# Retention: q of the last two heads made by seven-product jobs ahead, with the rotation of later k and q there

## The chip, the cores and the metric

The kernel runs on one core of a Trainium2 chip. The metric is the device time of one execution in microseconds. The core has a TensorE for matmuls (PE in the profile, PEld its weight loads), VectorE (DVE), ScalarE (ACT), GpSimd (POOL) and SyncE (SP), and 16 DMA engines. SP issues nearly all loads and stores, in its order; ScalarE and GpSimd have queues of their own.

## The reference

One inference step of a decoder with two layers: a short gated convolution with a SwiGLU, then retention with a SwiGLU. The change lies in the retention, which is computed for 512 prompt tokens and 32 sample tokens together (544 columns):

```python
def rotary(x, pos):                       # x1, x2: the two halves of 128
    return jnp.concatenate([x1 * cos - x2 * sin, x1 * sin + x2 * cos], axis=-1)

def retention_mixer(x, s0, pos, w_in, gn_g, w_out):
    q, k, v, g = jnp.split(x @ w_in, [QK_DIM, 2 * QK_DIM, 2 * QK_DIM + V_DIM], axis=-1)
    ...
    q = rotary(q, pos)
    k = rotary(k, pos) * (HEAD_DK ** -0.5)
    o, S = retention_chunkwise(q, k, v, s0)
    ...                                   # each head of o normalized: of
    out = (jax.nn.silu(g) * of) @ w_out
    return out, S
```

There are 4 heads; D_MODEL is 1024, a head has 256 columns of q and of k (two halves of 128 rows in the kernel) and 512 of v and of the gate g. Everything is float32.

## The kernel before

**Products.** Activations lie transposed, with channels on the partitions and 544 tokens along the free dimension. A float32 product is made of three matmuls on a high and a low part: high by high, high by low, low by high. `split` makes the parts, the high one by ScalarE (L204), the low one by VectorE (L205). A plain projection (`project`, L188) of 128 rows over 1024 channels has 8 channel tiles x 3 matmuls x 2 halves of 272 tokens: 48 matmuls. A projection of the retention's output (`held_project`) goes over one head's 512 channels, so it has 24.

**Seven-product jobs.** `Job` and `weights7` make a product of 256 rows by 1024 channels by 544 tokens with seven products of half size in place of eight: VectorE and ScalarE first form sums of the weights (L362 to L365, L337 to L339), GpSimd issues accumulating loads of low parts (L340), and `summed` adds the results up (ScalarE's copies for u1, u2 and p5, VectorE's additions L534 for c11, c12 and u3). A job has 7 x 4 x 3 = 84 matmuls of 272 columns (L424); as two plain projections it would be 96. `run` goes through a list of jobs; each prepares the weights of the next.

**Stages.** Convolution and its SwiGLU, up to 566 us; then `ahead`, which runs inside the end of that SwiGLU: it makes q and k of head 0 plainly, and then 11 jobs: the gates of all four heads (two jobs each) and k of heads 1, 2 and 3. What they make goes to DRAM (`qk_made`, `k_made`, `gate_made`) and is loaded back later. Work that a job leaves for later (`shaped`, the SiLU of a gate) is put in `pending` and issued at the next job's c11 (`flush`). Then come the four heads in turn, `last_project` and the second SwiGLU.

**A head.** `value` projects v (L1394 to L1396) in four groups; at group 1 it splits k and q of the head (`qk_split`) and, for heads 1 and 2, the gated output of the head before (`held_parts`). Then, woven by the order in which the loop of L1731 issues them and by `tc.issue_after`, which ties an issue behind an instruction: the loads of four sample-state tiles S (`states_load`), `state`, `scores`, `sample_outputs` (L1645), `states_update` (products L1663, VectorE's update L1669), `inner`, `normalized` and the gating (L1588). `fill(n)` puts the eight output projections of the older head between them, in pairs. While head h runs, its tail also makes q of head h + 1 by `qk_project` (two halves of 48 matmuls, each rotated as it comes out of PSUM, L1349), and rotates k of head h + 1 after its load (`rotate`, L1358 to L1366). Head 3 spreads the older head's projections over its own places and ends in `last_project`.

**Tiles.** `rot0` holds q, `rot1` holds k; `sqacc` and `sqlast` hold cos and sin; `qkhl1` is a tile of split parts; `gt`, `rot1`, `qkhl1` are reused in turn by the gate and by held parts. A tile can be written only when the last reader of what lay there is done.

## Time and profile before

| | us |
|---|---|
| median of 3 runs | 1382.14 (1382.0 to 1382.66) |
| span of the profiled execution | 1380.9 |
| TensorE busy | 1373.4 |
| VectorE busy | 1133.7 |
| `ahead`'s jobs | 566 to 682 |
| heads 0, 1, 2, 3 | from 682.0, 744.3, 831.4, 918.4 to 988.6 |

The span goes from the first to the last instruction of one execution on the chip that was taken with a profile. Engines run side by side, so an engine's busy time adds to the span only where nothing covers it. "Idle before, releaser" in a group's row says how long the engine had waited and for what. The chain of waits is followed back from the last instruction, step by step, to what released it.

### The profile page before, as it was taken

How to read it: one execution, taken by the hardware profiler on the slowest of the kernel's cores; microseconds unless marked ns; L12 is line 12 of the kernel's file. 1: busy time of each engine (PE TensorE's matmuls, PEld its weight loads, DVE VectorE, ACT ScalarE, POOL GpSimd, SP SyncE). 2: the span in 40 equal slices, each digit the busy share in tenths (PEclk: the TensorE clock that was granted, in tenths of full speed). 3: DMA queues.
4: the chain of work that ended last, by engine and by line, in shares of the span. 5: the costliest groups of instructions: out<-in, count | busy, mean ns of one | idle time of the engine just before them, and what ended most of it. 6: DMA issues, size and time to landing. Idle time of an engine off the chain costs nothing.

```text
span 1380.9 us, 26518 instructions
## 1 busy us (share of the span) xinstructions
PE 1373.4 (99%) x10420; PEld 1313.2 (95%) x10420; DVE 1133.7 (82%) x1929; ACT 822.6 (60%) x1288; POOL 212.1 (15%) x249
## 2 busy tenths in 40 slices
PE   9999999999999999999999999999999999999998
PEld 9999999999999999999978887887999999999998
DVE  6988889898989888777868576586799898989875
ACT  7666567677677656766631413224477767667654
POOL 0111011222222213211100000000112222221212
PEclk9999999999999999999999999999999999999999
DMA  6467347768676754777666455375757777777752
GB/s 225 121 157 169 110 108 172 171 165 187 145 191 151 166 123 128 189 202 208 189 231 229 146 186 205 134 260 184 225 126 161 171 177 171 157 180 164 166 112 88
DMA packets 99437, 232.89 MB, mean 169 GB/s; under 512 B 9808, under 2 KB 33888, under 8 KB 98928
## 3 DMA queue, kind: packets, MB, share of 16 engines
q1 hardware_dynamic: 68464, 167.26, 38.6%
q0 software_dynamic: 28400, 55.82, 23.4%
q10 hardware_dynamic: 2448, 8.12, 1.6%
q8 instruction: 81, 1.33, 0.4%
q14 instruction: 44, 0.36, 0.1%
HBM read 191.05 MB, written 28.42 MB: 159 GB/s over the span
## 4 chain that ended last, share of the span: by engine, by line
PE 99%; DVE 1%; issue 0%; DVEq 0%; ACT 0%
PE sm L424 45%; PE mm L424 16%; PE mm L188 16%; PE sm L188 6%; PE sm L1394 2%; PE sm L1395 2%; PE sm L1396 2%; PE sm L176 2%; PE sm L177 1%; PE sm L178 1%; PE sm L1645 1%; PE mm L1405 1%; PE mm L1573 1%; PE mm L1663 1%; PE sm L575 0%; PE mm L1464 0%
## 5 line engine op out<-in xcount | busy, mean ns | idle before, releaser
L424 PE MATMUL sm<-oh,wh 128*128 128x272 f32 x856 | 247.0, 289 | 0.0
L424 PE MATMUL sm<-ol,wh 128*128 128x272 f32 x856 | 246.2, 288 | 0.0
L424 PE MATMUL sm<-oh,wl 128*128 128x272 f32 x856 | 246.2, 288 | 0.0
L204 ACT ACTIVATE h<-w 128x512 fp32r<-128x512 f32 (+3 forms) x171 | 137.7, 805 | 90.5 <-PE mm L424 82.3
L205 DVE TENSOR_TENSOR l<-w,h 128x512 fp32r<-128x512 f32 (+3 forms) x171 | 154.6, 905 | 27.3 <-ACT h L204 25.1
L337 ACT ACTIVATE wh<-w 128x1024 fp32r<-128x1024 f32 (+1 forms) x133 | 132.9, 999 | 53.5 <-PE sm L424 40.0
L424 PEld LDWEIGHTS sm<-oh,wh 128*128 128x128 f32 x856 | 161.3, 188 | 0.6 <-DVE b L534 0.3
L424 PEld LDWEIGHTS sm<-oh,wl 128*128 128x128 f32 x856 | 161.1, 188 | 0.1
L424 PEld LDWEIGHTS sm<-ol,wh 128*128 128x128 f32 x856 | 160.8, 188 | 0.0
L424 PE MATMUL sm<-parts,wh 128*128 128x272 f32 x736 | 142.2, 288 | 0.0
L204 ACT ACTIVATE wh<-w 128x1024 fp32r<-128x1024 f32 (+3 forms) x80 | 69.0, 873 | 118.2 <-PE mm L188 61.2
L340 POOL DMA_DIRECT2D wl<-in_ffgu_dram x87 | 81.7, 939 | 323.5 <-ACT wl L339 136.7
L424 PEld LDWEIGHTS sm<-parts,wh 128*128 128x128 f32 x736 | 115.3, 188 | 0.0
L424 PE MATMUL mm<-oh,h 128*128 128x272 f32 x396 | 113.9, 288 | 0.0
L424 PE MATMUL mm<-oh,l 128*128 128x272 f32 x396 | 113.4, 286 | 0.0
L424 PE MATMUL mm<-ol,h 128*128 128x272 f32 x396 | 113.2, 286 | 0.0
L424 PE MATMUL sm<-parts,wl 128*128 128x272 f32 x368 | 106.0, 288 | 0.0
L339 ACT ACTIVATE wl<-wh 128x512 fp32r<-128x512 f32 (+1 forms) x172 | 102.4, 595 | 2.2
L338 DVE TENSOR_TENSOR wl<-w,wh 128x512 fp32r<-128x512 f32 (+1 forms) x133 | 86.3, 649 | 13.4 <-ACT wh L337 13.0
L205 DVE TENSOR_TENSOR wl<-w,wh 128x1024 fp32r<-128x1024 f32 (+3 forms) x80 | 81.2, 1023 | 14.5 <-ACT wh L204 14.1
L188 PE MATMUL mm<-parts,wh 128*128 128x272 f32 x488 | 82.8, 291 | 0.0
L424 PE MATMUL sm<-oh,h 128*128 128x272 f32 x284 | 82.8, 291 | 0.0
(384 smaller groups left out, 3816.1 us busy)
## 6 DMA issues: line engine op xcount, KB each, us to landing
w<-in_ffgu_dram SPq DMA_DIRECT2D x66, 512.0 KB
wl<-in_ffgu_dram POOLq DMA_DIRECT2D x87, 256.0 KB, 5.5
S<-in_rets_dram SPq DMA_DIRECT2D x16, 1024.0 KB
out_rets_dram<-S SPq DMA_DIRECT2D x16, 1024.0 KB
w<-in_ffdn_dram SPq DMA_DIRECT2D x36, 384.0 KB
cb<-in_ffgu_dram SPq DMA_DIRECT2D x22, 512.0 KB
w<-in_cvin_dram SPq DMA_DIRECT2D x21, 512.0 KB
wl<-in_ffdn_dram POOLq DMA_DIRECT2D x48, 192.0 KB, 4.7
```

What stands on the lines that cost most here:

```text
L176: nc.tensor.matmul(out, lh, rh, start=start, stop=False, skip_group_check=True)
L188: last_product[0] = nc.tensor.matmul(half(pt, hf)[:, :HT], w[:, c], act[k][:, hf * HT : (hf + 1) * HT], start=(first and k == ks[0] and i ...
L204: h = nc.scalar.activation(dh, src, AF.Copy)
L205: last_low[0] = nc.vector.tensor_sub(dl, src, dh.bitcast(F32))
L337: nc.scalar.activation(wh, w, AF.Copy)
L338: last_mixed[0] = nc.vector.tensor_sub(wl[:, :n], w[:, :n], wh[:, :n].bitcast(F32))
L339: minus = nc.scalar.activation(wl[:, n:], wh[:, n:].bitcast(F32), AF.Copy, scale=-1.0)
L340: nc.gpsimd.dma_start(wl[:, n:], src[:, 1, :] if len(src.shape) == 3 else src[:, n:], accum_op=ALU.add)
L424: last = nc.tensor.matmul(out, w[:, c], b, start=(first and j == 0 and i == 0), stop=(j == len(self.ks) - 1 and i == 2), skip_group_check= ...
L1394: nc.tensor.matmul(out, xh[kt][:, ts_], wh[:, cw], start=(kt == 0), stop=False)
L1395: nc.tensor.matmul(out, xh[kt][:, ts_], wl[:, cw], start=False, stop=False)
L1396: last = nc.tensor.matmul(out, xl[kt][:, ts_], wh[:, cw], start=False, stop=(kt == KT - 1))
```

## The change

- `ahead` runs 13 jobs instead of 11: q of heads 2 and 3 is now made by jobs of its own, (2, "q") and (3, "q"), and `qk_project` is called only in head 0, for q of head 1.
- k of heads 1 to 3 and q of heads 2 and 3 are rotated in `ahead` before they go to DRAM (`turn`, put in `pending`), with two temporaries from the pool `fp`. cos and sin are loaded after the first job. The mark `whole` stays only on the last two jobs.
- `sqacc` and `sqlast` become the halves of one tile, `squares`, which holds k of heads 2 and 3 once cos and sin are no longer needed.
- The gate of every head is loaded before `fill(2)`, from head 1 on into `qkhl1`. `held_parts` runs at group 1 of `value` for heads 1, 2 and 3 alike.
- The older head's projections stand singly in heads 1 and 2: 0, 1, 2, then 3 and 4; 5 in the place of q's first half, 6 in that of its second, and 7 behind it. Head 3 keeps its places.
- The made q of heads 2 and 3 is loaded at the end of the head before.

`rotate` and `turned` move up unchanged from the retention to a place ahead of `ahead`, and are left out here.

```diff
...
+QAHEAD = (2, 3)
...
-    sqacc = resid.tile([P, T], F32, tag="sqacc", name="sqacc")
-    sqlast = resid.tile([P, T], F32, tag="sqlast", name="sqlast")
+    squares = resid.tile([P, 2, T], F32, tag="squares", name="squares")
+    sqacc, sqlast = squares[:, 0, :], squares[:, 1, :]
...
     k_made = {h: dram.tile([P, 2, T], F32, tag=f"k{h}", name=nm("km")) for h in range(1, NH)}
+    q_made = {h: dram.tile([P, 2, T], F32, tag=f"q{h}", name=nm("qm")) for h in QAHEAD}
     gate_made = {h: dram.tile([P, 4, T], F32, tag=f"g{h}", name=nm("gm")) for h in range(NH)}
...
-            def k(what, src):
+            def qk(what, src):
                 g = tile2()
...
                     nc.scalar.activation(g[:, 1, :HT], src, AF.Copy)
-                    nc.scalar.dma_start(k_made[h], g)
-            if n is None:
-                return Job([a["rtqk"][h, 2 + i] for i in range(2)], operand, sw, summed(tile2, k), third, spare=spare(), first=0)
+                    def turn():
+                        two = [fp.tile([P, 5, HT], F32, tag="f", name=nm("rt")) for _ in range(2)]
+                        rotate(g, *[t[:, :2, :].rearrange("p a b -> p (a b)") for t in two])
+                        nc.scalar.dma_start((q_made if n == "q" else k_made)[h], g)
+                    pending.append(turn)
+            if n in ("q", "k"):
+                at = 2 * (n == "k")
+                return Job([a["rtqk"][h, at + i] for i in range(2)], operand, sw, summed(tile2, qk), third, spare=spare(), first=0)
-        jobs = [gates(*hn) for hn in ((0, 0), (0, 2), (1, None), (1, 0), (1, 2), (2, None), (2, 0), (2, 2), (3, None), (3, 0), (3, 2))]
+        jobs = [
+            gates(*hn)
+            for hn in (
+                (0, 0), (0, 2), (1, "k"), (1, 0), (1, 2), (2, "k"), (2, 0), (2, "q"), (2, 2), (3, "k"), (3, 0), (3, "q"), (3, 2)
+            )
+        ]
...
-        for one_job in (jobs[5], jobs[8], *jobs[-2:]):
+        for one_job in jobs[-2:]:
             one_job.places["whole"] = True
-        run(jobs, (2, 5, 6), lambda i: factors() if i == 1 else None, iter(()))
+        def after(i):
+            if i == 0:
+                with tc.issue_after(last_load[0].ins):
+                    for j, t in enumerate((cos, sin)):
+                        nc.sync.dma_start(t, a["rope"][j])
+            elif i == 1:
+                factors()
+        run(jobs, (2, 5, 6), after, iter(()))
...
-        cos, sin = sqacc, sqlast
-        for i, t in enumerate((cos, sin)):
-            nc.sync.dma_start(t, a["rope"][i])
...
-            return {"rot": [
-                pool.tile([P, 2, T], F32, tag=f"rot{w}", name=nm("rot"), bufs=1) for w, pool in enumerate((tp, kp))
-            ]}
+            rot = tp.tile([P, 2, T], F32, tag="rot0", name=nm("rot"), bufs=1)
+            return {"rot": [rot, squares if h in QAHEAD else kp.tile([P, 2, T], F32, tag="rot1", name=nm("rot"), bufs=1)]}
...
                 if c == 1:
-                    with tc.issue_after(last_normal[0].ins) if h else ExitStack():
-                        qk_split(h, st, 1)
+                    if h not in QAHEAD:
+                        with tc.issue_after(last_normal[0].ins) if h else ExitStack():
+                            qk_split(h, st, 1)
                     qk_split(h, st, 0)
...
                     keys(h, st, pvs[:, 1, P:])
-                    if h in AHEAD:
+                    if h:
                         held_parts(h, older)
+                    if h in QAHEAD:
+                        qk_split(h, st, 1)
...
         def held_parts(h, st):
-            if h in AHEAD:
-                yh = [kp.tile([P, 2, T], F32R, tag=t, name=nm("oldh"), bufs=1) for t in ("gt", "rot1")]
-                yl = swapped(h == 2, [P, 4, T], F32R, "oldl")
-                for i, t in enumerate(yh):
-                    c = slice(2 * i, 2 * i + 2)
-                    split(t, yl[:, c, :], st["gate"][0][:, c, :])
-                held["y"] = [t[:, n, :] for t in yh for n in range(2)], [yl[:, n, :] for n in range(4)]
-            else:
-                for n in range(4):
-                    split(xh[n], xl[n], gate_tile(st, n))
-                held["y"] = xh[:4], xl[:4]
+            yh = [kp.tile([P, 2, T], F32R, tag=t, name=nm("oldh"), bufs=1) for t in ("gt", "rot1")]
+            yl = swapped(h > 1, [P, 4, T], F32R, "oldl")
+            for i, t in enumerate(yh):
+                c = slice(2 * i, 2 * i + 2)
+                split(t, yl[:, c, :], st["gate"][0][:, c, :])
+            held["y"] = [t[:, n, :] for t in yh for n in range(2)], [yl[:, n, :] for n in range(4)]
...
-            def fill(n):
-                if h in AHEAD:
-                    for i in range(2):
-                        held_project(h, (0, 4, 2, 6)[n] + i)
-                        if n == i == 0:
-                            st["placed"]()
-                elif not more and n % 2:
-                    if n == 1:
-                        held_parts(h, older)
-                    held_project(h, 2 + n // 2)
+            def fill(place):
+                for n in {1: ((0,), (1,), (2,), (3, 4)), 2: ((0,), (1,), (2,), (3, 4)), 3: ((), (2,), (), (3,))}.get(h, ((),) * 4)[place]:
+                    held_project(h, n)
+                    if n == 0:
+                        st["placed"]()
...
                 scores(h, st, c)
-            if h == 0:
-                st["gate"] = [swapped(True, [P, 4, T], F32, "gate")]
-                nc.sync.dma_start(st["gate"][0], gate_made[0])
+            st["gate"] = [qp.tile([P, 4, T], F32, tag="qkhl1", name=nm("gate"), bufs=1) if h else swapped(True, [P, 4, T], F32, "gate")]
+            nc.sync.dma_start(st["gate"][0], gate_made[h])
             fill(2)
...
             first = first or [inner(h, st, it) for it in range(2)]
-            if h in AHEAD:
-                st["gate"] = [swapped(h == 2, [P, 4, T], F32, "gate")]
             if more:
...
                 states_load(h, st, 3)
-            if h in AHEAD:
-                with tc.issue_after(st["loaded"].ins):
-                    nc.sync.dma_start(st["gate"][0], gate_made[h])
-            elif not more:
-                st["gate"] = [
-                    pool.tile([P, 2, T], F32, tag=t, name=nm("gate"), bufs=1) for pool, t in ((qp, "qkhl1"), (kp, "gt"))
-                ]
-                for i, t in enumerate(st["gate"]):
-                    nc.sync.dma_start(t, gate_made[h][:, 2 * i : 2 * i + 2, :])
             yn0 = normalized(first[0], fe[:, 0, h : h + 1])
...
             states_update(h, st, 1)
-            if more:
-                with tc.issue_after(last_update[0].ins):
-                    rotate(nxt["rot"][1], *products())
             sample_outputs(h, st, 2)
...
             with tc.issue_after(last_product[0].ins):
-                if more:
+                if h == 0:
                     qk_project(h + 1, nxt, 0, 0)
                 else:
-                    held_project(h, 4)
+                    held_project(h, 5 if more else 4)
             with tc.issue_after(last_product[0].ins):
...
-            if more:
+            if h == 0:
                 qk_project(h + 1, nxt, 0, 1, inside)
+            elif more:
+                nc.sync.dma_start(nxt["rot"][0], q_made[h + 1])
+                held_project(h, 6, single=True, weave=(None, inside))
+                held_project(h, 7)
             else:
...
                 held_project(h, 0, False, single=True, weave=iter((inside,)))
```

The first order is VectorE's in `ahead`, around the job (2, "q"), whose result is gate_8047. Before, at the end of the job of k of head 2 (gate_7771), with sums of weights (w, L362 to L365) and low parts (wl, l) of later jobs:

```order
L534 TENSOR_TENSOR gate_7771<-gate_7771,mm_7842 128x272
L205 TENSOR_TENSOR l_939_7826<-w_931_7802,h_938_7825 128x512
L338 TENSOR_TENSOR wl_7940<-w_7930,wh_7939 128x512
L205 TENSOR_TENSOR l_950_7942<-w_945_7931,h_949_7941 128x1024
L534 TENSOR_TENSOR gate_7901<-gate_7901,sm_7986 128x272
```

After, at the end of the job of q of head 2:

```order
L536 TENSOR_TENSOR gate_8047<-gate_8047,mm_8118 128x272
L1117 TENSOR_TENSOR rt_8276<-gate_8047,squares 128x544
L207 TENSOR_TENSOR l_976_8102<-w_968_8078,h_975_8101 128x512
L1118 TENSOR_TENSOR gate_8047<-gate_8047,squares 128x544
L340 TENSOR_TENSOR wl_8215<-w_8205,wh_8214 128x512
L1119 TENSOR_TENSOR rt_8275<-gate_8047,squares 128x544
L1120 TENSOR_TENSOR gate_8047<-gate_8047,squares 128x544
L1124 TENSOR_TENSOR gate_8047<-gate_8047,rt_8275 128x544
L207 TENSOR_TENSOR l_987_8217<-w_982_8206,h_986_8216 128x1024
L536 TENSOR_TENSOR gate_8177<-gate_8177,sm_8261 128x272
L340 TENSOR_TENSOR wl_8225<-cb,wh_8224 128x512
L1125 TENSOR_TENSOR gate_8047<-gate_8047,rt_8276 128x544
```

The six operations of the rotation now stand between the splits of the next job's weights.

The second is VectorE's at the start of head 0, after the small operations of the setup (put is the last). Before, k of head 0 (rot_8571) has been rotated further up, and only its low part and the rotation of q (rot_8570) stand here:

```order
L1327 TENSOR_TENSOR put<-cb 128x128
L1215 TENSOR_TENSOR gate_8405<-gate_8405,R 128x1088
L205 TENSOR_TENSOR qkhl_8681<-rot_8571,qkhl_8681 128x1024
L1358 TENSOR_TENSOR rt_8602<-rot_8570,sqlast 128x544
L1360 TENSOR_TENSOR rt_8601<-rot_8570,sqlast 128x544
```

After, with k as rot_8867 and q as rot_8866:

```order
L1360 TENSOR_TENSOR put<-cb 128x128
L207 TENSOR_TENSOR wl_9024<-w_9022,wh_9023 128x1024
L1232 TENSOR_TENSOR gate_8699<-gate_8699,R 128x1088
L1117 TENSOR_TENSOR rt_1053_8883<-rot_8867,squares 128x272
L1119 TENSOR_TENSOR rt_1053_8883<-rot_8867,squares 128x272
L1118 TENSOR_TENSOR rot_8867<-rot_8867,squares 128x272
L1120 TENSOR_TENSOR rot_8867<-rot_8867,squares 128x272
L1124 TENSOR_TENSOR rot_8867<-rot_8867,rt_1053_8883 128x272
L1125 TENSOR_TENSOR rot_8867<-rot_8867,rt_1053_8883 128x272
L1117 TENSOR_TENSOR rt_8898<-rot_8866,squares 128x544
L1117 TENSOR_TENSOR rt_1054_8890<-rot_8867,squares 128x272
```

A split of value weights and the rotation of k in two halves now come ahead of the rotation of q.

The third place is the end of head 1. On TensorE, the values of head 2 (L1394 to L1396 before, L1415 to L1417 after) begin there. Before, they follow the last matmuls of q of head 2 (sm_9917, sm_9918):

```order
L188 MATMUL sm_9918<-parts,wh_9912 128x272
L188 MATMUL sm_9917<-parts,wl_9913 128x272
L188 MATMUL sm_9918<-parts,wl_9913 128x272
L1394 MATMUL sm_9990<-wh_9996,parts 128x512
L1395 MATMUL sm_9990<-wl_9997,parts 128x512
```

After, with L1597 as a transposition of normalized rows, L1687 as the two products of the last state tile (mm_10102, mm_10103), and sm_10080 and sm_10081 as the halves of projection 6 of the older head:

```order
L1597 MATMUL sm_10094<-cb,yn_10046 128x128 x4
L1687 MATMUL mm_10102<-vs_9713,kns_9582 128x512 x2
L190 MATMUL sm_10081<-oldh_9589,wh_10075 128x272
L190 MATMUL sm_10080<-oldl_9590,wh_10075 128x272
L1687 MATMUL mm_10103<-vs_9713,kns_9582 128x512 x2
L190 MATMUL sm_10081<-oldl_9590,wh_10075 128x272
L190 MATMUL sm_10080<-oldh_9589,wl_10076 128x272
L190 MATMUL sm_10081<-oldh_9589,wl_10076 128x272
L1415 MATMUL sm_10151<-wh_10157,parts 128x512
L1416 MATMUL sm_10151<-wl_10158,parts 128x512
```

Projection 6 ends there in place of q, with the products of the last state tile five matmuls before its end, and projection 7 follows after the first eight matmuls of the values.

On VectorE in the same tail, from the second update of state tile 2 on. Before (rot_9732 is k, rot_9731 q of head 2):

```order
L1669 SCALAR_TENSOR_TENSOR S_9388<-S_9388,mm_9903 128x1024
L1588 TENSOR_TENSOR gate_9730<-gate_9730,sm_9955 128x4x128
L1550 TENSOR_SCALAR yn_9961<-sm_9860,mv_9887,rs_9888 128x512
L1669 SCALAR_TENSOR_TENSOR S_9734<-S_9734,mm_9963 128x1024
L1669 SCALAR_TENSOR_TENSOR S_9734<-S_9734,mm_9964 128x1024
L1349 TENSOR_TENSOR rt_9845<-sm_9917,sqlast 128x272
L1349 TENSOR_TENSOR rt_9845<-sm_9918,sqlast 128x272
L1349 TENSOR_TENSOR rot_9731<-sm_9917,sqacc 128x272
L1349 TENSOR_TENSOR rot_9731<-sm_9918,sqacc 128x272
L1365 TENSOR_TENSOR rot_9731<-rot_9731,rt_9845 128x544
L1366 TENSOR_TENSOR rot_9731<-rot_9731,rt_9846 128x544
```

After (rot_9936 is the made q of head 2, x the residual):

```order
L1693 SCALAR_TENSOR_TENSOR S_9676<-S_9676,mm_10065 128x1024
L1612 TENSOR_TENSOR gate_9818<-gate_9818,sm_10094 128x4x128
L1574 TENSOR_SCALAR yn_10100<-sm_10022,mv_10049,rs_10050 128x512
L1693 SCALAR_TENSOR_TENSOR S_9938<-S_9938,mm_10102 128x1024
L1693 SCALAR_TENSOR_TENSOR S_9938<-S_9938,mm_10103 128x1024
L318 TENSOR_TENSOR x_80<-x_80,sm_10080 128x272
L318 TENSOR_TENSOR x_80<-x_80,sm_10081 128x272
L207 TENSOR_TENSOR qkhl_10231<-rot_9936,qkhl_10231 128x1024
L1444 SCALAR_TENSOR_TENSOR qm<-rot_9936,gs_10234 128x4x4 x3
L318 TENSOR_TENSOR x_81<-x_81,mm_10125 128x544
```

The rotation of q out of PSUM is gone, and the additions of projections 6 and 7 stand there.

More of the change, by code (lines that the diff above doesn't have):

```diff
@@ L1107, in hybrid_decode_kernel, with rotate, turned @@
     k_made = {h: dram.tile([P, 2, T], F32, tag=f"k{h}", name=nm("km")) for h in range(1, NH)}
+    q_made = {h: dram.tile([P, 2, T], F32, tag=f"q{h}", name=nm("qm")) for h in QAHEAD}
     gate_made = {h: dram.tile([P, 4, T], F32, tag=f"g{h}", name=nm("gm")) for h in range(NH)}
+    cos, sin = sqacc, sqlast
+    def rotate(r, t0, t1, c=slice(0, T)):
+        nc.vector.tensor_mul(t1, r[:, 0, :], sin[:, c])
+        nc.vector.tensor_mul(r[:, 0, :], r[:, 0, :], cos[:, c])
+        nc.vector.tensor_mul(t0, r[:, 1, :], sin[:, c])
+        nc.vector.tensor_mul(r[:, 1, :], r[:, 1, :], cos[:, c])
+        turned(r, t0, t1)
+    def turned(r, t0, t1):
+        nc.vector.tensor_sub(r[:, 0, :], r[:, 0, :], t0)
+        nc.vector.tensor_add(r[:, 1, :], r[:, 1, :], t1)
     def ahead(tp, fp, sw, operand_tiles, wp):
```

9 lines of the change are left out of this document (removed).

## The prediction

> **What bounds the kernel now.** I read the page's busy line and its chain first, to see which engine sets the end:
>
> ```profile
> PE 1373.4 (99%) x10420; PEld 1313.2 (95%) x10420; DVE 1133.7 (82%) x1929; ACT 822.6 (60%) x1288; POOL 212.1 (15%) x249
> PE 99%; DVE 1%; issue 0%; DVEq 0%; ACT 0%
> ```
>
> TensorE is busy for 1373.4 of 1380.9 us, and the chain that ends last lies on it for 99%. So time goes only if matmuls go, and time comes only if TensorE is made to wait. The list of waits, asked for TensorE alone, has one entry:
>
> ```profile
> PE sm L575 <- DVE expo L109: 1.1, 1, 1.1
> ```
>
> That wait is at the start of the program, far from the change. Then I cut the span by stage and by head (columns: sum of the stretch, busy time and count of PE, PEld, DVE, ACT, POOL, the granted clock, the DMA share, GB/s):
>
> ```profile
> 566.00:686.00 120.00, 120.00 (x940) 118.85 (x940) 89.11 (x149) 82.11 (x131) 17.91 (x24) 1.00 0.69 189
> ...
> 682.00:744.30 62.30, 62.30 (x366) 47.90 (x365) 47.90 (x83) 21.10 (x33) 7.58 (x13) 1.00 0.70 235
> 744.30:831.40 87.10, 87.10 (x566) 72.75 (x565) 60.76 (x95) 24.16 (x33) 2.65 (x5) 1.00 0.54 184
> 831.40:918.40 87.00, 87.00 (x565) 72.65 (x564) 60.80 (x95) 24.03 (x32) 2.65 (x5) 1.00 0.54 187
> 918.40:988.60 70.20, 70.20 (x430) 55.42 (x429) 51.79 (x90) 22.07 (x32) 3.62 (x6) 1.00 0.61 207
> ```
>
> The first row is the seven-product jobs of `ahead`, the others are heads 0 to 3. In all five TensorE has no gap. VectorE is at 74% in `ahead` and at 70% in heads 1 and 2: it is the engine that can fall behind.
>
> **The matmuls.** A busy time per matmul must not be used here, since neighbours overlap:
>
> ```profile
> L188 PE MATMUL mm<-parts,wh 128*128 128x272 f32 x160 | 26.9, 289 | 0.0
> ```
>
> 289 ns is what one takes from start to end. What a removed one gives back is the step from one to the next, and the chain has it (start, length, count): first three pieces of a seven-product job, then the two halves of q's projection, that of head 0 and that of head 1.
>
> ```profile
> 618.71 3.02 PE sm L424 x24
> 621.73 1.51 PE mm L424 x12
> 623.24 4.49 PE sm L424 x36
> ...
> 726.11 6.02 PE mm L188 x48
> ...
> 813.24 6.01 PE mm L188 x48
> ```
>
> A plain projection of one half of q is 48 matmuls in 6.02 us, 125.4 ns each. Heads 1 and 2 each lose two halves: 4 x 48 = 192 matmuls, 4 x 6.02 = 24.1 us. In the jobs 72 matmuls take 9.02 us, 125.3 ns each; a job has seven products of 12, so 84 matmuls and 10.52 us. Two are added: 168 matmuls, 21.0 us. **The path of TensorE gets shorter by 24 matmuls, 3.0 us.** The rest of its work is only placed anew: the eight projections of the older head stay 24 matmuls (3.0 us) each. The second half of q, which was woven with other work, hands its place to the projection `held_project` 6, of the same form, so what the weaving costs stays.
>
> The Trainium skill, page "TensorE: Matmul & The Clock Gate", section "Back-to-back issue gap", gives the isolated warm gap as N / 2.4 + 2.5 ns; for 272 columns my estimate by it is 115.8 ns, and the gain would be 2.8 us. The rows above show 125.4 ns, at a granted clock of 1.00, and the sum goes by them.
>
> **VectorE in `ahead`.** Five rotations come in here (k of heads 1 to 3, q of heads 2 and 3), six operations of 128x544 each. Before, one of them is on the timeline at the tail of head 1 (start, length):
>
> ```profile
> 812.91 0.72 DVE L1358 TENSOR_TENSOR rt<-rot,sqlast 128x544 f32<-128x544 f32 x1
> 813.55 0.72 DVE L1360 TENSOR_TENSOR rt<-rot,sqlast 128x544 f32<-128x544 f32 x1
> ...
> 816.09 0.71 DVE L1366 TENSOR_TENSOR rot<-rot,rt 128x544 f32<-128x544 f32 x1
> 816.73 0.69 DVE L1536 BATCH_NORM_STATS2 bst<-sm 128x6 f32<-128x512 f32 x1
> ```
>
> From 812.91 to 816.73: 3.8 us for one rotation, 19.1 us for five. The stage had 89.1 us of VectorE in 11 jobs, 8.1 us a job; two more bring 16.2 us, and the rotation of k of head 0, which leaves the stage, takes 4.2 us away. That is 120 us of VectorE in 141 us, 85%. It does not lie evenly: a job of q or k has 8.1 + 3.8 = 11.9 us of VectorE behind 10.5 us of TensorE and falls 1.4 us behind; the gate job after it has 8.1 us and regains 2.4. The cover is that order: apart from the first, every second job is one of gates. VectorE also had time to wait there:
>
> ```profile
> L534 DVE TENSOR_TENSOR gate<-gate,sm 128x272 f32<-128x272 f32 x22 | 9.5, 434 | 6.1 <-PE sm L424 5.8 <-ACT wl L339 0.3
> ```
>
> Its additions waited 5.8 us for TensorE, so it was ahead of it then. I take nothing here; without that reserve it is 5 x 1.4 = 7.0 us, and it can't be below nothing, since TensorE had no wait in this stage to lose. The stores of k and q go out on ScalarE's queue, and the added jobs' weights come on SP's and POOL's queues in their order and at the jobs' own pace of 10.5 us, as those of the other jobs did.
>
> **The start of head 0.** k of head 0 was loaded early and rotated on VectorE beside the last jobs, in 12 operations on half tiles from 668.8 to 674.1:
>
> ```profile
> 668.82 0.43 DVE L1358 TENSOR_TENSOR rt<-rot,sqlast 128x272 f32<-128x272 f32 x1
> 669.17 0.43 DVE L1360 TENSOR_TENSOR rt<-rot,sqlast 128x272 f32<-128x272 f32 x1
> ...
> 673.76 0.43 DVE L1366 TENSOR_TENSOR rot<-rot,rt 128x272 f32<-128x272 f32 x1
> ```
>
> Now its tile shares memory with a temporary of the rotation of q of head 3, and the load comes behind that. Its rotation then stands at the head's start, between these rows of before:
>
> ```profile
> 682.53 1.29 DVE L1215 TENSOR_TENSOR gate<-gate,R 128x1088 f32<-128x1088 f32 x1
> 683.74 1.22 DVE L205 TENSOR_TENSOR qkhl<-rot,qkhl 128x1024 fp32r<-128x1024 f32 x1
> 685.27 0.73 DVE L1358 TENSOR_TENSOR rt<-rot,sqlast 128x544 f32<-128x544 f32 x1 [0.32 <-DMA rot<-qkm]
> ...
> 688.46 0.72 DVE L1366 TENSOR_TENSOR rot<-rot,rt 128x544 f32<-128x544 f32 x1
> ...
> 695.56 0.19 DVE L1619 TENSOR_TENSOR ss<-mm,mput 128x32 f32<-128x32 f32 x1 [3.67 <-PE mm L1614]
> ```
>
> and on TensorE's chain:
>
> ```profile
> 694.99 0.46 PE mm L1614 x4
> ...
> 708.36 0.43 PE sm L176
> ```
>
> In the frame of before: a split of value weights (1.2 us) and the gate's product (1.2) end at 684.9; 12 operations on halves of k at 0.35 us from start to start make 4.2, q's rotation 3.8, the low part of k 1.1: q is ready at 694.1, where L1614 wants it at 695.0. Before, q was done at 689.2, with some 6 us to spare; now 0.9 are left. I take nothing. The bounds are nothing and 4.2 us, the whole rotation of k, if its load lands that late. Behind it on VectorE stand the low part of q (1.2 us) and the small operations for the sample states; the products that use them begin after the values, at 708 us, so a delay of 1 us there is covered.
>
> **The tails of heads 1 and 2.** Before, the stretch from the third state update to the next head's values was covered on TensorE by q's projection, 12.0 us; now by held projections 5, 6 and 7, 9.0 us. VectorE loses there one rotation of k and one of q (7.6 us) and gets three additions to the residual:
>
> ```profile
> L1669 DVE SCALAR_TENSOR_TENSOR S<-S,mm 128x1024 f32<-128x1024 f32 x32 | 38.1, 1211 | 1.2 <-PE mm L1663 1.2
> L316 DVE TENSOR_TENSOR x<-x,mm 128x544 f32<-128x544 f32 x19 | 13.7, 719 | 21.1 <-PE mm L188 21.1
> ```
>
> three at 0.72 us, 2.2 us. So VectorE is eased by 5.4 us and TensorE by 3.0; in sum the tail is not tighter. But single places are: the second product of state tile 2, the second normalization and both products of tile 3 now stand 2 to 4 us apart on TensorE, where VectorE has two updates of 1.2 us, a normalization and a gating of 0.7 us each between them. Adding these durations up in the order of both engines, I place each of these, as an estimate, within 0.1 to 0.4 us of its need. The price if one update is late is 1.2 us a head, 2.4 in all. On the other side, before, projections stood in pairs, the second waiting for the first's addition: two of them took 3.22 and 3.18 us instead of 24 x 0.1254 = 3.01:
>
> ```profile
> 771.29 3.22 PE mm L188 x24
> ...
> 775.44 3.18 PE mm L188 x24
> ```
>
> 0.2 us each, two such in both heads, 0.8 us at most to gain. I take +0.2 us, between these ends and near to nothing, since the large sums balance.
>
> **Loads, and head 3.** Heads 1 and 2 now last 75 us each. They moved 184 GB/s x 87.1 us = 16.0 MB; without q's weights (1.0 MB) and with the made q (0.6) it is 15.6 MB, 207 GB/s over 75 us; head 0 ran at 235. Two loads are placed anew on SP's queue. The gate (1.1 MB, 6 us at that rate) now stands ahead of the head's state tile 3, which used to go first: at most 6 us later, with no wait of TensorE for a state before. The made q stands behind the next head's state tile 0, and on VectorE the addition of projection 7 and the last gating wait behind its split. The nearest row is what the made k cost VectorE as a load in three heads:
>
> ```profile
> L1358 DVE TENSOR_TENSOR rt<-rot,sqlast 128x544 f32<-128x544 f32 x4 | 2.9, 722 | 2.2 <-DMA rot<-km 1.9 <-DMA rot<-qkm 0.3
> ```
>
> 1.9 us of VectorE, 0.6 a head, none of it on the path. For both I take nothing, with the price of a tail as their bound. Head 3 has one gating operation in place of two and splits its held tiles earlier: nothing to 0.5 us gained, I take nothing.
>
> **Sum.** 1380.9 - 24.1 + 21.0 + 0.2 = 1378.0 us of span. The median of the runs, 1382.14, is 1.24 us above the profiled span, so **1379.3 us**: 2.8 us less, 0.21%. About 0.2%, 2.8 us, is what a measurement of this kernel can tell from no change, so the forecast lies just at that edge.
>
> **Rivals.**
> - The lost cover turns into waits: one update late in both tails (2.4 us), or the start of head 0 late by its reserve again (0.9 us). For it: reserves of 0.1 to 0.9 us where there were 6 and more. Against it: VectorE's sum in the tails falls. It gives 1379.1 + 0.9 to 2.4, some 1380 to 1381.5: no difference that can be told. Chance 0.41.
> - VectorE becomes the bound in `ahead`, and it ends slower: each of the five q and k jobs is 1.4 us late because a rotation stands in front of a split that the next product needs, and the gate jobs do not win it back for TensorE. 1379.1 + 7.0 = 1386.1 us. It decides once the reserve of those splits is under 1.4 us. Against it are the 5.8 us of waiting above. Chance 0.08.
> - The start of head 0 is late by all of k's rotation, 4.2 us: 1383.3, on the edge of slower. Chance 0.04, half of it slower.
> - The rotations hold up POOL: both their inputs lie in SBUF. If each of 30 operations stopped POOL for its 0.72 us, its accumulating loads of low weights would come 21.6 us late in all, at most 1400.7 us. Chance 0.02. This is a rule of the Trainium skill (page "SBUF — State Buffer", section "Who interferes with whom": a two-input operation of VectorE from SBUF contends with GpSimd instructions that read SBUF); no row of before shows such a stop.
> - A removed matmul is worth its whole 289 ns: 24 x 0.289 = 6.9 us, 1375.2 us. The chain's 125 ns speak against it. Chance 0.02.
> - The change doesn't do what it says: the heads still hold q's products. The order shows them gone; no chance is given.
>
> **How the numbers follow.** The forecast (gain of 2.8 to 3.5 us) has 0.43, the waits 0.41, the rest 0.16 as above (0.01 of it for nothing named, slower). Faster by over 0.2%: 0.43 + 0.02 = 0.45; slower: 0.08 + 0.02 + 0.02 + 0.01 = 0.13; within: 0.42. The range starts at 1378.0 (1379.1 less 0.8 in the tails and part of head 3's 0.5) and ends at 1383.0 (1379.1 with 2.4 in the tails, 0.9 at head 0 and some more); it leaves out the 289 ns, the slower cases and a little of the waits, 2 in 10.
>
> **What would show it.** The jobs' stage is 21 us longer with TensorE busy throughout; heads 1 and 2 take 75.0 us each, head 0 62.3. Wrong would be (lines of the changed kernel): a wait of TensorE for the splits L340 or L207 in `ahead`; for the rotation L1124 or L1125 at L1638; for the update L1693 or the gating L1612 between a head's last state and the next value L1415; or chain pieces of 12 matmuls in `ahead` longer than 1.51 us.

## The result, and the profile after

| | before | changed kernel |
|---|---|---|
| median, us | 1382.4 (1382.0 to 1382.67, 4 runs) | 1393.34 (1392.58 to 1395.63, 4 runs) |
| span of the profiled execution | 1380.9 | 1391.8 |

The ratio is 1.008, 95% interval [1.0066, 1.0094]: slower by 10.9 us where 2.8 us less were forecast. The page of the changed kernel, busy line and chain:

```profile
PE 1376.3 (99%) x10396; PEld 1313.6 (94%) x10396; DVE 1141.3 (82%) x1938; ACT 832.5 (60%) x1304; POOL 216.0 (16%) x255
...
PE 96%; DVE 2%; DMA 1%; ACT 1%; issue 0%; SPq 0%; DVEq 0%; ACTq 0%
```

The 24 matmuls are gone (10420 to 10396 in the records). But TensorE holds 96% of the chain in place of 99%, and the list of waits of TensorE (us in total, times, longest) has new entries:

```profile
PE sm L426 <- ACT oh L206: 6.5, 3, 5.5
...
PE sm L426 <- DVE ol L207: 0.9, 2, 0.7
PE sm L1597 <- DVE yn L1574: 0.4, 2, 0.2
PE sm L1416 <- DVE wl L207: 0.2, 1, 0.2
```

L426 is the matmul of the seven-product jobs. To see which jobs, I cut both spans at the same events: the first matmul of `ahead`'s jobs, the first value matmul of each head, the first matmul of the last SwiGLU and its last seven-product matmul. The windows of before, the jobs of `ahead` and then head 3 and the last SwiGLU (length in us, then busy time and count of PE, PEld, DVE, ACT, POOL, the granted clock, DMA share, GB/s):

```profile
565.30:681.90 116.60, 116.60 (x929) 116.18 (x927) 86.05 (x145) 78.94 (x124) 13.97 (x17) 1.00 0.68 188
...
918.40:1018.70 100.30, 100.30 (x669) 85.45 (x668) 77.73 (x135) 48.31 (x68) 7.68 (x11) 1.00 0.64 197
1018.70:1345.90 327.20, 327.20 (x2620) 326.88 (x2619) 292.60 (x517) 225.51 (x358) 66.60 (x77) 1.00 0.71 161
```

And of the changed kernel, all stages:

```profile
564.70:702.10 137.40, 137.40 (x1097) 137.09 (x1096) 112.66 (x181) 91.11 (x145) 19.42 (x25) 1.00 0.73 195
702.10:764.50 62.40, 62.40 (x366) 47.87 (x366) 48.74 (x93) 21.94 (x34) 6.08 (x13) 1.00 0.67 236
764.50:837.80 73.30, 72.88 (x445) 57.82 (x444) 51.41 (x83) 21.95 (x30) 2.65 (x5) 1.00 0.58 201
837.80:913.70 75.90, 75.68 (x470) 60.98 (x468) 51.07 (x80) 22.15 (x30) 2.65 (x5) 1.00 0.57 203
913.70:1017.60 103.90, 103.71 (x693) 88.61 (x691) 67.72 (x107) 39.45 (x53) 7.94 (x11) 1.00 0.65 201
1017.60:1357.00 339.40, 332.11 (x2618) 330.39 (x2619) 301.88 (x535) 234.83 (x371) 66.33 (x76) 0.98 0.67 155
```

| stage, us | before | changed | difference |
|---|---|---|---|
| `ahead`'s jobs | 116.6 | 137.4 | +20.8 |
| head 0 | 62.4 | 62.4 | 0 |
| heads 1, 2, 3 and `last_project` | 274.4 | 253.1 | -21.3 |
| last SwiGLU, to its last seven-product matmul | 327.2 | 339.4 | **+12.2** |

The first two rows are as forecast (+21.0 and 0), the third should have been -23.9 (24.1 less the 0.2 for the tails). The fourth is a stage that the prediction does not mention, in which the change edits nothing.

What happened at its start is read from the chain of waits of the changed kernel (start, length, what):

```profile
990.44 23.73 PE mm L190 x189
1014.17 0.02 issue
1014.19 0.28 ACT wh L339
1014.47 0.69 issue
1015.15 0.73 ACT f L884
...
1021.80 2.47 DVE ol L207 x3
...
1029.12 0.64 DVE ol L207
1029.76 0.04 issue
1029.81 1.27 PE sm L426 x4
```

Before, the same chain goes from one matmul stage to the next without leaving TensorE:

```profile
991.96 26.95 PE mm L188 x215
1018.90 8.77 PE sm L424 x69
```

f (L884, L882 before) is the scratch tile in which the SwiGLU scales the residual and from which ScalarE and VectorE split the operands oh and ol of its first products. When it was written is a view of that one line (count, duration min/median/max, first and last start). Before, then the changed kernel:

```profile
L882 ACT ACTIVATE f<-x,vec x8: 733/737/752, 992.7 to 1020.7; 128x544 f32<-128x544 f32 x8
```

```profile
L884 ACT ACTIVATE f<-x,vec x6: 732/735/749, 1015.2 to 1024.0; 128x544 f32<-128x544 f32 x6
```

Before, the first operands were made beside the last projections, from 992.7 us on; now the first f comes at 1015.2, after `last_project` has last read the held parts (1014.2 on TensorE), and most of the operands are made on ScalarE and VectorE with TensorE waiting.

### The profile page after: what moved, and what is told of

The parts are those of the page before. It is cut to its first block, busy times and chain, and to the rows that moved or that the text cites. A ratio compares the mean times of both kernels' runs of the same rounds, so it can differ in the third digit from the quotient of the medians.

```text
span 1391.8 us, 26526 instructions
## 1 busy us (share of the span) xinstructions
PE 1376.3 (99%) x10396; PEld 1313.6 (94%) x10396; DVE 1141.3 (82%) x1938; ACT 832.5 (60%) x1304; POOL 216.0 (16%) x255
## 3 DMA queue, kind: packets, MB, share of 16 engines
q0 software_dynamic: 29264, 57.40, 24.1%
## 4 chain that ended last, share of the span: by engine, by line
PE 96%; DVE 2%; DMA 1%; ACT 1%; issue 0%; SPq 0%; DVEq 0%; ACTq 0%
PE sm L426 45%; PE mm L426 17%; PE mm L190 14%; PE sm L190 5%; PE sm L1416 2%; PE sm L1417 2%; PE sm L1415 2%; PE sm L178 2%; PE sm L179 1%; PE sm L180 1%; PE sm L1669 1%; DMA x<-in_xT_dram 1%; PE mm L1426 1%; PE mm L1597 1%; PE mm L1687 0%; DVE ol L207 0%
## 5 line engine op out<-in xcount | busy, mean ns | idle before, releaser
L426 PE MATMUL sm<-oh,wh 128*128 128x272 f32 x872 | 252.5, 290 | 6.5 <-ACT oh L206 6.5
L426 PE MATMUL sm<-ol,wh 128*128 128x272 f32 x872 | 252.1, 289 | 1.0 <-DVE ol L207 0.9
L426 PE MATMUL sm<-oh,wl 128*128 128x272 f32 x872 | 251.3, 288 | 0.0
L339 ACT ACTIVATE wh<-w 128x1024 fp32r<-128x1024 f32 (+1 forms) x138 | 138.2, 1001 | 62.4 <-PE sm L426 45.4
L426 PEld LDWEIGHTS sm<-oh,wh 128*128 128x128 f32 x872 | 165.1, 189 | 7.4 <-ACT oh L206 7.2
L426 PEld LDWEIGHTS sm<-ol,wh 128*128 128x128 f32 x872 | 164.6, 189 | 1.9 <-DVE ol L207 1.8
L426 PEld LDWEIGHTS sm<-oh,wl 128*128 128x128 f32 x872 | 164.9, 189 | 0.0
L426 PE MATMUL sm<-parts,wh 128*128 128x272 f32 x768 | 148.3, 288 | 0.0
L206 ACT ACTIVATE wh<-w 128x1024 fp32r<-128x1024 f32 (+3 forms) x74 | 63.2, 860 | 126.8 <-PE mm L190 86.7
L426 PEld LDWEIGHTS sm<-parts,wh 128*128 128x128 f32 x768 | 120.3, 188 | 0.0
L426 PE MATMUL mm<-oh,h 128*128 128x272 f32 x404 | 116.2, 288 | 0.0
L426 PE MATMUL mm<-oh,l 128*128 128x272 f32 x404 | 115.7, 286 | 0.0
L426 PE MATMUL mm<-ol,h 128*128 128x272 f32 x404 | 115.4, 286 | 0.0
L426 PE MATMUL sm<-parts,wl 128*128 128x272 f32 x384 | 110.4, 288 | 0.0
L426 PE MATMUL sm<-oh,h 128*128 128x272 f32 x292 | 85.7, 294 | 0.0
L426 PE MATMUL sm<-ol,h 128*128 128x272 f32 x292 | 84.9, 291 | 0.0
L426 PE MATMUL sm<-oh,l 128*128 128x272 f32 x292 | 84.6, 290 | 0.0
```

Source lines behind the costliest of these rows:

```text
L206: h = nc.scalar.activation(dh, src, AF.Copy)
L339: nc.scalar.activation(wh, w, AF.Copy)
L426: last = nc.tensor.matmul(out, w[:, c], b, start=(first and j == 0 and i == 0), stop=(j == len(self.ks) - 1 and i == 2), skip_group_check= ...
```

## The experiments

**Theory A**: the change moves head 3's held parts from the resident tiles to `gt`, `rot1` and the tile of `gate`; in the built program f lies on the addresses of `gt` and `rot1`, and projection 7, which reads the held parts, is among the last of `last_project`. So f must wait. In before the held parts lay in resident tiles (`xh`, `xl`), on which f does not lie. One rival puts the loss on what an idle TensorE does to its own clock; another, rival L below, on what the heads do with the late tiles, wherever the SwiGLU's tiles lie.

**E1: head 3's held parts back in the resident tiles.** The rest of the change stays (the gate of head 2 takes another tile, so that head 3's is free).

```diff
-                    if h:
+                    if h in AHEAD:
                         held_parts(h, older)
...
         def held_parts(h, st):
+            if h not in AHEAD:
+                for n in range(4):
+                    split(xh[n], xl[n], gate_tile(st, n))
+                held["y"] = xh[:4], xl[:4]
+                return
...
             def fill(place):
+                if not more and place == 1:
+                    held_parts(h, older)
```

> The changed kernel with one part undone: head 3 splits the older head's output into the resident tile (xh, xl), behind its first state products, as before the change; the gate of head 2 goes to the tile of low values for that. The rest of the change stays. Theory A (the temporaries f of the last SwiGLU lie in the memory of gt and rot1, where head 3's held parts now live up to projection 7, so the operands of its first jobs start 22 us late): the wait of TensorE for oh at the start of that SwiGLU (6.5 us) goes, the granted clock stays at 1.00 there, and of the 12.2 us lost in that stage nearly all come back: 1381 us, 1380 to 1382.5. Theory B (the stage lost its time because sums of squares share a tile with k, or through the order of ScalarE, whatever lies in gt and rot1): little changes, 1391 to 1394 us.

**E2: before, with the late tiles alone.** None of the change but this: head 3's high held parts go to `gt` and `rot1`. As `gt` is taken then, head 3's gate, which had lain in `qkhl1` and `gt`, lies whole in `qkhl1`.

```diff
-                for n in range(4):
-                    split(xh[n], xl[n], gate_tile(st, n))
-                held["y"] = xh[:4], xl[:4]
+                yh = [kp.tile([P, 2, T], F32R, tag=t, name=nm("oldh"), bufs=1) for t in ("gt", "rot1")]
+                for i, t in enumerate(yh):
+                    for n in range(2):
+                        split(t[:, n, :], xl[2 * i + n], gate_tile(st, 2 * i + n))
+                held["y"] = [t[:, n, :] for t in yh for n in range(2)], xl[:4]
...
```

> The kernel before with only this of the change: head 3 keeps the high parts of the older head's output in gt and rot1, up to projection 7, and its gate whole in qkhl1. No matmul is moved or removed. Theory A: a wait for oh of 5 to 7 us at the start of the last SwiGLU, a lower granted clock behind it, and 10 to 13 us more than before: 1393 to 1396 us. Theory B: as before, 1382 to 1383 us.

E1: 1381.9 us (1380.53 to 1383.37), ratio to before 0.9997 [0.9988, 1.0007]. E2: 1394.97 us (1394.12 to 1396.18), ratio 1.0091 [1.0074, 1.0108]. The last SwiGLU in E1, then in E2 with its new wait:

```profile
1017.90:1345.20 327.30, 327.30 (x2621) 326.98 (x2620) 292.78 (x517) 225.59 (x358) 66.59 (x77) 1.00 0.71 161
```

```profile
1018.70:1358.00 339.30, 331.82 (x2617) 329.88 (x2616) 301.78 (x536) 235.58 (x373) 66.90 (x77) 0.98 0.69 155
```

```profile
PE sm L424 <- ACT oh L204: 6.5, 3, 5.5
```

Undoing that one part takes the 12 us away, and that part alone brings them to the kernel before, with the same wait to a tenth.

**E3: TensorE kept busy.** The changed kernel with 60 matmuls that nothing reads, put ahead of the SwiGLU's first products.

```diff
+    def keep_busy(n):
+        pt = bank()
+        for i in range(n):
+            nc.tensor.matmul(pt[:, :HT], xh[0][:, :P], xh[1][:, :HT], start=True, stop=True)
...
+            if layer == 1:
+                keep_busy(60)
```

> The changed kernel with 60 matmuls added that nobody reads (7.5 us at 125 ns), between the last projection of the retention and the first matmul of the last SwiGLU, where TensorE otherwise waits for operands. Theory A with a clock that falls after such a wait: the added matmuls lie in time that was waiting, the granted clock stays at 1.00, and the 4 to 5 us that the slow steps of 230 ns cost mostly come back: 1389 to 1391.5 us. If the clock has no share in it: the same as the changed kernel or up to 2 us slower, 1393 to 1396 us.

1392.81 us (1391.73 to 1393.81), ratio 1.0075 [1.006, 1.009], which can't be told from the changed kernel; it lies 0.2 us under the range for a clock without a share and 1.3 above the other. The granted clock is the third number from the end; first the changed kernel, then E3. The last row of each is the stretch from the 21st product matmul of the stage to the 45th:

```profile
1020.00:1026.00 6.00, 0.46 (x5) 0.24 (x3) 5.89 (x12) 5.67 (x10) 0.86 (x1) 0.67 0.28 46
1026.00:1030.00 4.00, 3.03 (x9) 2.07 (x10) 4.00 (x9) 3.78 (x6) 0.00 (x0) 0.50 0.15 26
1030.00:1034.00 4.00, 3.97 (x17) 3.65 (x17) 3.24 (x6) 2.23 (x5) 0.00 (x0) 0.50 0.00 0
...
1029.81:1035.77 5.96, 5.93 (x25) 5.61 (x26) 5.17 (x9) 3.08 (x6) 0.00 (x0) 0.51 0.00 0
```

```profile
1020.00:1026.00 6.00, 6.00 (x50) 6.00 (x49) 5.99 (x12) 5.68 (x9) 0.86 (x1) 1.00 0.28 45
1026.00:1030.00 4.00, 2.81 (x20) 2.32 (x19) 3.91 (x8) 3.78 (x7) 0.00 (x0) 1.00 0.43 65
1030.00:1034.00 4.00, 3.27 (x18) 2.84 (x19) 3.24 (x7) 2.69 (x6) 0.00 (x0) 0.81 0.00 0
...
1030.83:1035.97 5.14, 4.90 (x24) 4.68 (x25) 4.35 (x8) 2.96 (x6) 0.00 (x0) 0.67 0.00 0
```

The waits are 7.4 us of the 12.2; the other 4.8 looked like matmuls at half clock. Up to 1030 us these are not a cost of their own. VectorE is busy for nearly all of 1020 to 1030 us in both kernels (5.89 and 4.00 us, 5.99 and 3.91), and the 21st product matmul, which waits for VectorE's last late operand, starts 12.2 us into the stage in the changed kernel and 12.5 us into it in E3, where the clock stood at 1.00: the making of the operands sets this time, and slow matmuls ahead of it lay where TensorE would else have waited.

Behind it the chain lies on TensorE, and there the clock counts. In before the 21st matmul started 2.5 us into its stage, so the changed kernel is 9.7 us late at that point. The next 24 matmuls then take 5.96 us in place of 3.15 in before, at a clock of 0.51: 2.8 us more. Some 0.3 is won back later, which gives the 12.2. E3 does not test that part, since its clock fell there too (0.67 in its last row) and its 24 matmuls took 5.14 us. So the clock alone does not make the loss, which begins with the late operands; but some 2.8 us of it are, as an estimate, half clock that followed the wait.

**E8: the SwiGLU's scratch elsewhere.** The heads of the changed kernel; only the pools of the last SwiGLU are opened in another order, so that f lies on neither `gt` nor `rot1`.

```diff
-            fp = c1.enter_context(tc.tile_pool(name=f"ffp{layer}", bufs=2, reuse_waits="tile"))
-            one = c1.enter_context(tc.tile_pool(name=f"ffo{layer}", bufs=1, reuse_waits="tile"))
-            lp = c1.enter_context(tc.tile_pool(name=f"ffl{layer}", bufs=1, reuse_waits="tile"))
+            places = {}
+            for t in ("lof", "fol")[1 - layer]: places[t] = c1.enter_context(tc.tile_pool(name=f"ff{t}{layer}", bufs=1 + (t == "f"), reuse_waits="tile"))
+            fp, one, lp = places["f"], places["o"], places["l"]
```

> The changed kernel, with the heads as they are: only the SwiGLU behind the heads has its pools opened in another order, so that its scratch tile f and the operands of its first input tile lie apart from the memory of head 3's held parts; the operands of the second input tile still overlap the low held parts, and those of the last lie on the high ones. Theory A (the memory that head 3's held parts keep until 1014 us makes the first products wait): the scratch tile is written before 1010 us and the wait of 6.5 us ahead of the first product shrinks by at least 2 us; what stays is what is overlapped still, and the time is 1383 to 1390 beside the changed kernel's 1393.3. Rival L (the later writing of the held parts in head 3, or the order of the weights there, delays the SwiGLU, wherever its tiles lie): the wait stays at 11 us in all, the time at 1392 to 1394.

1392.08 us (1391.73 to 1392.97), ratio 1.007 [1.0055, 1.0086]. f does come early, but the wait shrinks by 1.4 us only, not by 2, and the time lies in the range of rival L:

```profile
L884 ACT ACTIVATE f<-x,vec x7: 734/751/752, 991.6 to 1024.4; 128x544 f32<-128x544 f32 x7
...
PE sm L426 <- ACT oh L206: 5.1, 1, 5.1
```

That is a miss. The operands still came after 1014 us. The low held parts lie on the second input tile's operands, which is a second overlap in the changed kernel, and on ScalarE the first split of an operand (oh) stood behind a weight split (wh) that waits for the projections (start, length, what, idle before and its releaser):

```profile
1014.66 1.06 ACT L339 ACTIVATE wh<-w 128x1024 fp32r<-128x1024 f32 x1 [4.92 <-PE mm L190]
1015.63 0.64 ACT L206 ACTIVATE oh<-f 128x544 fp32r<-128x544 f32 x1
```

E8 can't separate theory A from rival L, so the next pair leaves the low parts in resident tiles.

**E9: the same question as a pair.** Both are E1 with the high held parts alone in `gt` and `rot1` (E2's edit); the second also has E8's order of pools.

> E1 with the high held parts of head 3 alone written to the two late tiles that the changed kernel uses (the low parts stay in the resident tiles); the last SwiGLU's pools as they are. Theory A: its scratch tile lies on the high parts, which projection 7 reads to its end, so the wait ahead of the SwiGLU is back at 6 to 7 us in the operands' splits and the stretch from there to the last seven-product matmul is 339.3 us, as in E2, the time 1393 to 1395. Rival L (the low parts' tile): no wait, 1381.9.

> The run beside it, with the same heads and the SwiGLU's pools opened in the other order of E8: now only the operands of the last input tile lie on the high held parts. Theory A (an address, not the held parts' time or place in the heads): the wait is gone but for under 1 us, the stretch 327 to 328.5 us, the time 1381.5 to 1383.5. Rival L (what the heads do with the late tiles delays the SwiGLU by another way, such as the order of the splits on ScalarE): the wait stays at over 4 us and the time at 1391 to 1395.

The first: 1393.88 us (1393.29 to 1395.01), ratio 1.0079 [1.0064, 1.0094]. The second: 1382.28 us (1381.0 to 1383.54), ratio 0.9997 [0.9987, 1.0006]. The last SwiGLU in the one and in the other:

```profile
1017.20:1356.70 339.50, 332.25 (x2618) 330.51 (x2619) 301.83 (x535) 234.91 (x371) 66.42 (x76) 0.98 0.68 155
```

```profile
1017.20:1344.40 327.20, 327.20 (x2620) 326.89 (x2620) 292.56 (x517) 225.53 (x358) 66.63 (x77) 1.00 0.71 161
```

The heads are the same; in the source only the order of the SwiGLU's pools differs, and with it the addresses, and all 12.3 us go. So it is the overlap, and neither the late writing of the held parts nor their use. The order of instructions that the build makes follows the overlap too: in the first f stands on ScalarE behind a weight split (wh) that runs at 1013.8 us, in the second ahead of it, from 991.1 us on. How much the wait for the memory and how much this order costs was not separated; both come with the overlap. What the low held parts, which in E8 still overlap an operand, cost by themselves was not tried.

**E4 to E7: the other 3 us.** With the overlap gone, E1 still does not show the whole gain of the matmuls. Its heads, with the waits of TensorE in them:

```profile
764.20:838.20 74.00, 73.01 (x445) 57.86 (x444) 51.46 (x83) 22.03 (x30) 2.65 (x5) 1.00 0.57 199
838.20:913.70 75.50, 75.47 (x467) 60.92 (x465) 50.80 (x78) 22.13 (x30) 2.67 (x5) 1.00 0.58 202
913.70:1017.90 104.20, 104.16 (x693) 88.63 (x694) 77.50 (x129) 48.32 (x68) 7.68 (x11) 1.00 0.65 200
...
PE sm L1416 <- DVE wl L207: 0.8, 1, 0.8
PE sm L1597 <- DVE yn L1574: 0.2, 1, 0.2
```

What they should be follows from before: 12.0 us of q go from heads 1 and 2, and projection 7, 3.0 us, now lies behind the next head's first value matmuls: 87.1 - 15.0 = 72.1, 87.0 - 12.0 = 75.0, 100.3 + 3.0 = 103.3. E1 is above that by 1.9, 0.5 and 0.9 us.

E4 is E1 with the work inside projection 6 woven in one step later (`weave=(None, None, inside)`).

> As e1_parts_again, and in the tails of heads 1 and 2 the gating of row block 2, the last normalization and the products of state tile 3 are woven into projection 6 one step (6 matmuls) later. If the 0.38 us in front of the transposition of yn in both tails are a wait for VectorE that 6 matmuls (0.75 us) cover, and nothing behind becomes late: 0.5 to 0.8 us under e1_parts_again. If the chain behind it is as tight: 0 to 0.5 us over it.

1381.81 us (1380.62 to 1382.91), 0.9998 [0.9989, 1.0007]. The built order of instructions was E1's, so it says nothing on the tail; it is a second measurement of E1.

E5 is E1 with the load of the made k behind that of the made q. The load of state tile 3, which had been tied behind k's, is untied by the same edit; head 1's last state load is issued at 828.6 us in E1 and at 828.7 in E5.

```diff
-                k_loaded = nc.sync.dma_start(nxt["rot"][1], k_made[h + 1])
-            with tc.issue_after(k_loaded.ins) if h in AHEAD else ExitStack():
-                states_load(h, st, 3)
+                if h not in AHEAD:
+                    nc.sync.dma_start(nxt["rot"][1], k_made[h + 1])
+            states_load(h, st, 3)
...
                 q_loaded = nc.sync.dma_start(nxt["rot"][0], q_made[h + 1])
+                with tc.issue_after(q_loaded.ins):
+                    nc.sync.dma_start(nxt["rot"][1], k_made[h + 1])
```

> E1 (head 3's held parts back in the resident tiles) with one more change: the made k of heads 2 and 3 is loaded behind the made q, in the tail of the head before, and no longer in that head's value. Theory K: in E1 head 1's value waits 0.8 us in TensorE (for the low part of a value weight from VectorE), because that weight's load is issued as before, 13.2 us into the value, but shares the DMA engines with the k load just ahead of it and two state loads. Then the wait goes, and the profiled span is some 0.8 to 1.0 us below E1's 1380.0, the time 1380.8 to 1381.2 beside E1's 1381.9. Rival S: the two state loads alone make the weight late. Then the wait at the low part stays at 0.8 us and the time at 1381.9. Rival T: k arrives too late for its split in the tail; then a new wait of 1 to 3 us for the parts of k stands ahead of scores of heads 2 and 3, and the time is 1383 to 1385.

1381.1 us (1380.4 to 1382.16), 0.9992 [0.9983, 1.0001]; the span, 1380.1, is not below E1's 1380.0, since the stages ahead of the jobs took 1.2 us more in that execution; head 1 is 72.9 us in place of 74.0, and the other heads and the last SwiGLU differ by 0.1 at most:

```profile
765.50:838.40 72.90, 72.68 (x446) 57.98 (x445) 51.33 (x83) 21.94 (x30) 2.66 (x5) 1.00 0.58 202
```

E1's queue of SP at the start of head 1 shows the load of k that E5 takes away from there (start, length), and ScalarE what came late:

```profile
766.46 5.38 SPq L1657 DMA_DIRECT2D S<-in_rets_dram  x2
771.89 0.50 SPq L1795 DMA_DIRECT2D squares<-km  x1
777.40 0.34 SPq L160 DMA_DIRECT2D w<-in_rtv_dram  x1
```

```profile
783.40 1.06 ACT L206 ACTIVATE wh<-w 128x1024 fp32r<-128x1024 f32 x1 [1.71 <-DMA w<-in_rtv_dram]
```

Without k's load that wait of ScalarE and the wait at L1416 are gone. So theory K holds, of a size of 1 us, read from one profile of each; the medians of E1 and E5 are 0.8 us apart, within the spread of their runs. In before the load of this k was issued at 808.6 us, 64 us into head 1, and in E1 it is issued 8 us into it: its new tile, `squares`, comes free earlier than `rot1` did, and so the load reached the place where a weight's load was needed.

E6 is E5 with the last transposition, the gating and the last update behind all of projection 6 in the tails of heads 1 and 2; E7 has that in head 1's alone.

```diff
-                held_project(h, 6, single=True, weave=(None, inside))
+                held_project(h, 6, single=True, weave=(None, inside) if h == 2 else ())
+                if h == 1:
+                    inside()
                 held_project(h, 7)
```

> E5 with one more change: the last transposition of output, the gating and the last state update of heads 1 and 2 stand behind all 24 matmuls of held projection 6 in place of after its 16th. Theory W: E1's tails lose some 0.4 us a head where TensorE waits for VectorE's normalization of the sample output ahead of a transposition, and some 0.5 us a head in single products of the last state tile placed apart among the projection. Then both shrink, and the time is 0.5 to 1.5 us below E5's. Rival V: the work that stood behind the transposition is then late for the next head's value or for held projection 7, and a new wait of the same size or more stands there: the time is E5's or up to 1.5 us above it.

> E5 with E6's edit at the tail of head 1 alone. In E6 the tail of head 1 was 0.9 us shorter than in E5, and head 3 had a new wait of 1.2 us in its value that E5 has not. If that wait hangs on the edit in head 2's tail: the time from the first match of the jobs ahead to the last SwiGLU is some 2.0 us below the kernel before (E5: 1.1 below), the time 1380.0 to 1380.4 beside 1382.2 of before, and faster than both kernels. If it hangs on head 1's tail: the wait is there again and the time is E6's, 1381.1.

E6: 1381.15 us (1380.23 to 1382.29), 0.999 [0.9981, 0.9999]: head 1 is 0.9 us shorter than in E5, but head 3 is 1.8 us longer, with a new wait of 1.2 us at the split of the values (vh and vl, 0.4 and 0.8). The time is E5's, as rival V had it. E7: 1380.8 us (1379.88 to 1381.23), **0.9986 [0.9977, 0.9995]**. That wait is not in E7, but a smaller one for a state tile is, in head 3. Its heads and its waits in them:

```profile
765.00:837.00 72.00, 72.00 (x445) 57.86 (x443) 50.42 (x82) 21.49 (x28) 2.66 (x5) 1.00 0.58 203
837.00:912.60 75.60, 75.54 (x468) 60.94 (x466) 50.48 (x78) 21.00 (x29) 2.68 (x5) 1.00 0.56 196
912.60:1017.40 104.80, 104.19 (x693) 88.60 (x694) 78.52 (x130) 49.56 (x71) 7.69 (x11) 1.00 0.67 205
...
PE sm L1669 <- DMA S<-in_rets_dram: 0.6, 1, 0.6
```

E7 is faster than both kernels, by 1.4 us than before; the range expected, 1380.0 to 1380.4, was missed, and the stretch from the jobs to the last SwiGLU is 1.3 us shorter than before, not 2.0. The gain is small, but each of its 11 runs lies below each of the 15 of before beside it (1381.65 and up). Head 1 is now what its matmuls say, 72.0. Heads 2 and 3 are 0.6 and 1.5 us above; 0.6 of it is the wait shown. What holds the rest, about 1.5 us, was not settled.

## Why the prediction was wrong

- **The matmuls: right.** `ahead` grew by 20.8 us where 21.0 were forecast, head 1 of E7 fell by 15.1 where 12.0 + 3.0 were. The step of 125 ns from the chain held. By the estimate of 115.8 ns for an isolated matmul, from the Trainium skill, page "TensorE: Matmul & The Clock Gate", section "Back-to-back issue gap", 168 matmuls would have been 19.5 us, less than the stage grew by.
- **VectorE in `ahead`: taken at nothing, right.** It was busy for 112.66 of 137.4 us, and TensorE for all of it, with no wait there. The rival at 1386.1 us did not come about, and the one on POOL would have shown as a wait of TensorE in this stage, which there was not.
- **The start of head 0: taken at nothing, right.** 62.4 us, no wait: the reserve of 0.9 us was enough.
- **The tails, +0.2 us with -0.8 and 2.4 as ends: mis-sized.** Heads 1 to 3 fell by 21.3 us in place of 24.1, a loss of 2.8. The rival of the lost cover had 2.4 us for this, which is near by chance: its late updates (L1693) were not seen, and what the tails show is 0.4 us of waiting for the normalization yn, and 0.9 us that E6 took off head 1 by another order there. E5 shows 1 us of E1's loss to be the made k's load. The prediction knew that load only as a wait of VectorE in before (1.9 us) and did not have it among the loads that are placed anew. In the changed kernel the wait at L1416 was 0.2 us, not E1's 0.8, so its share of the 2.8 there was not measured. That heads 1 and 2 would take 75.0 us each was wrong by its cut: projection 7 of head 1 is counted behind the cut, and 73.3 and 75.9 were measured.
- **Head 3: the step that failed.** It read "splits its held tiles earlier: nothing to 0.5 us gained, I take nothing". It weighed the work of the splits and not where they are kept and until when. The prediction used the rule that a tile is written only when the last reader of its memory is done for k of head 0, and did not put the same question to head 3, where the next owner of the memory is the SwiGLU. The term that it put at nothing cost 12.2 us there, shown in E1, E2 and the pair E9: the operands of the SwiGLU came late because their scratch tile lay on the held parts.
- So 1378.0 us of span, forecast, + 12.2 in the SwiGLU + 2.6 in the heads (2.8 less the 0.2 taken) = 1392.8; measured were 1391.8. Of the 1.0 us between, 0.6 is the start, 565.3 before and 564.7 now, 0.2 the jobs, and 0.2 what follows the last seven-product matmul (35.0 before, 34.8 now).

## What to carry to other kernels

When a change keeps a tile longer or in another place, follow its memory to the next owner, also into a later stage that the change does not touch: ask who writes there next, and whether that write made operands in the shade of the last matmuls. A stage whose first operands are made beside the end of the one before has a lead that no busy time shows; it is seen only in when its first scratch tile is written. And a load whose tile comes free earlier is issued earlier: see which load of that queue is needed next there.

## What the runs showed of the hardware

After the wait of 5.5 us in the changed kernel the granted clock was 0.50 for 1026 to 1034 us, and matmuls of 272 columns stood 0.23 us apart in place of 0.125. The Trainium skill, page "TensorE: Matmul & The Clock Gate", section "What's actually happening", has half clock after an idle window of some 3.4 us, and the row agrees. In E3 no wait there was longer than 1.2 us, and the clock still fell, to 0.81 in 1030 to 1034 us and 0.67 in 1030.83 to 1035.97; the window that the page names is longer than any of these waits, so it does not account for this fall, and what did was not tried.

The same half clock cost nothing that can be measured while VectorE's operands were the bound, up to 1029.8 us, and an estimated 2.8 us of the 12.2 behind that, where 24 matmuls took 5.96 us in place of 3.15. So this wait of TensorE cost more than its own length, by the matmuls at half clock that came after the operands were there.
